# A two-layer encoder step on one core: loads and splits beside the attentions kept in program order, later marks, two more pairs of keys moved, a longer lead

## The chip, the core and the metric

The kernel runs on one core of a Trainium2 chip. The metric is device time in microseconds (us) from start to end of one launch, less being better. The core has a matrix engine (PE; its weight loads are listed as PEld), three elementwise engines (DVE, ACT, POOL), and SP, whose queue issues most DMA transfers. Every engine runs its own instruction stream in order, and semaphores tie the streams together. All engines share the on-chip memory SBUF; matmuls write to PSUM.

## What is computed

Two layers over 2048 prompt frames and 64 sample frames, width 1024, 16 heads of 64. Layer A attends over a band of chunks with softmax, layer B over all earlier frames with stick-breaking weights. Cut to the core of the reference:

```python
h = rms_norm(x, norm_a);  q, k, v, gate = split(h @ w_in_a, 4)
s = q @ k.T * SCALE + rel_bias;  p = softmax(where(mask, s, NEG_INF))   # band: own chunk + 8 before
x = x + ((p @ v) * silu(gate)) @ w_out_a
kb, vb = split(rms_norm(x, norm_kv) @ w_kv, 2)                          # shared by layer B
q, gate = split(rms_norm(x, norm_b) @ w_in_b, 2)
z = q @ kb.T * SCALE                                                    # strictly causal
log_fail = where(mask, log_sigmoid(-z), 0)
later = flip(cumsum(flip(log_fail))) - log_fail
w = where(mask, exp(log_sigmoid(z) + later), 0)
x = x + ((w @ vb) * silu(gate)) @ w_out_b
y = rms_norm(x, norm_f)
```

The sample frames also attend to cached keys and values, and the new keys and values are outputs too.

## The kernel before

**Precision.** All products are made from float32 values that are split in a high and a low part, each in the form that PE takes at full rate, and summed over three matmuls: high times high, high times low, low times high. So every operand costs a pass on ACT (the high part, a rounded copy) and one on DVE (the low part, the difference). These passes are the *splits* or *cuts*.

**Stages.** (1) Projection A makes k, q, v, gate of layer A: `ps_t` matmuls with the weights `wh`, `wl`, from 50 us to 750 us. (2) Attention A goes over eight head pairs in two halves of the frames, 763 to 1330 us; (3) the last output tiles of layer A (`ps_o`) run to 1455 us. (4) Projections for the shared keys and values and for layer B follow, to 2060 us. (5) Attention B (`z`, `f`, scans, `wt`, `acc`), 2070 to 3250 us. (6) The last output tiles of layer B.

**Attention.** Scores `z` are made by PE. In A, DVE adds the bias and takes the maximum, ACT makes the exponential `s`; in B, ACT makes `f`, POOL and DVE scan it to `s`. PE turns the weights over (`wt`), ACT and DVE split them (`ph`, `pl`), and PE multiplies them with the values (`acc`). One such round over a tile is a *beat* of the class `Beat`.

**Work beside the attention.** PE would wait for the elementwise engines in an attention, so `Beat` puts other matrix work between the beats, one *step* (six matmuls) at a time, `RATE` steps a beat: first *late jobs* (`late_job`), the projections of the second half of the frames for head pairs named in `DEFER` (tiles `lraw`, `lwh`, `lwl`, `ps_j`); then the splits of the output weights (`w_out_steps`: `woraw` to `big`); then the output tiles (`out_tile`: it loads the attention's output `og` and the residual `xr`, splits `og` in `oh` and `ol`, multiplies with the output weights in `ps_o`). Each has parts *ahead* (load and cuts), products, and parts *behind*. `Beat.lead(n)` runs n products before the first beat. An output tile may start when its frames' sums are written, which `when_summed` marks some beats later. A late job's load is traced with the first product of the job before it, and its cuts, each of `STEP` = 2 of eight blocks, with the products of that job's second half.

**What sets the order.** The program is traced once, and the tile framework then orders each engine's stream by itself, by its own estimate of when things are ready. A class `InOrder` can tie an instruction behind the one traced before it on the same engine (`keep_in_program_order`), but only while its flag `on` is set, and in this kernel it never is. The queue of SP holds the loads of q (L427), keys (L442), values (L448), the writes of the attention's output (L529), `lraw` (L641), `woraw` (L707), `og` (L736) and `xr` (L738).

**Between the layers.** `normed` loads a tile `xt`, squares it into a scrap tile `junk` on ACT, whose sum gives `rstd`; the scaled tile is transposed into `ps_tr` and split into `x_own`, which `ps_v` multiplies. `junk` takes its buffer from the pool tag of the residual `xr` (2 buffers).

Of the kernel before, what the change touches and what calls it, by code (L numbers as in the profile page):

```python
# [38 lines left out]

SAMPLE = {(1, 0): [4, 3], (3, 2): [2, 1, 0]}  # L40

DEFER = dict(a=[("k", 6), ("k", 7)], b=[(k, hp) for k in "gq" for hp in range(HP)])

RATE = dict(a=0.4, b=0.3)
LAG = dict(a=2, b=5)

LEAD = dict(a=8, b=8)
HOLD = dict(a=1, b=2)

STEP = 2  # L50
TOK = [(t * P, min(P, T - t * P)) for t in range((T + P - 1) // P)]

HALF = NP // 2
# [18 lines left out]
class InOrder:  # L72


    def __init__(self, tc):
        self.tc, self.on = tc, False

    def engine(self, engine):
        outer = self
# [17 lines left out]
def encoder_step(ctx: ExitStack, tc: tile.TileContext, a: dict, o: dict):  # L97
    nc = tc.nc
    order = InOrder(tc)
    dve, act, gps, pe = (order.engine(x) for x in (nc.vector, nc.scalar, nc.gpsimd, nc.tensor))  # L100
    mm = pe.matmul

    cpool = ctx.enter_context(tc.tile_pool(name="consts", bufs=1))
    dram = ctx.enter_context(tc.tile_pool(name="scratch", bufs=1, space=DRAM))
# [86 lines left out]
    def projections(L, x_of, begin, w_v, cv, gv, out_v, jobs, first, prompt, sample, stages):  # L191
        with (
# [1 line left out]
            tc.tile_pool(name=f"pp_{L}", bufs=1, space=PSUM) as psum,  # L194
        ):


            x_own = [xpool.tile([P, NK, HALF + m], F32R, name=f"x_own{i}") for i, m in enumerate((2 * NS, NS))]
            x_big = big_pair()
            xs = [x_own, x_big]  # L200
            with tc.tile_pool(name=f"v_{L}", bufs=2) as pool:

                def normed(t, scale=gps.tensor_scalar):
                    r0, n = TOK[t]
                    xt = pool.tile([P, D], F32, name="xt", tag="xt", bufs=3)
                    nc.sync.dma_start(xt[:n], x_of(t))
                    junk = opool.tile([P, D], mybir.dt.bfloat16, name="junk", tag="xr", bufs=2)
                    r = rstd_of(pool, xt, n, junk)
                    scale(xt[:n], xt[:n], r[:n], 1.0, ALU.mult, ALU.mult)
                    ps = psum.tile([P, NK, P], F32, name="ps_tr", tag="tr", bufs=1)  # L210
                    for k in range(NK):
                        flip(ps[:, k, :n], xt[:n, k * P : (k + 1) * P])
                    hf, c = spot(r0)
                    split(*(x[:, :, c : c + n] for x in xs[hf]), ps[:, :, :n])
                    if n == NS:
                        act.activation(x_own[0][:, :, NEW + NS :], f32(x_own[1][:, :, NEW:]), AF.Copy)

                seq = [t for gs_ in ORDER for g in gs_ for t in range(4 * g, 4 * g + 4)] + [len(TOK) - 1]
                if L == "a":
                    seq.sort()  # L220
                normed(seq[0], dve.tensor_scalar)
                begin()
                for half in range(2):
                    wh, wl = [], []
                    for k in range(NK):
                        raw = pool.tile([P, CH], F32, name="vraw", tag="vraw", bufs=2)
                        c = cv + half * CH
                        nc.sync.dma_start(raw, w_v[k * P : (k + 1) * P, c : c + CH])
                        h_ = pool.tile([P, CH], F32R, name="vwh", tag=f"vwh{k}", bufs=1)
                        l_ = pool.tile([P, CH], F32R, name="vwl", tag=f"vwl{k}", bufs=1)  # L230
                        act.activation(h_, raw, AF.Copy, scale=gv[:, k : k + 1])
                        dve.scalar_tensor_tensor(
                            l_, raw, gv[:, k : k + 1], f32(h_), ALU.mult, ALU.subtract
                        )
                        wh.append(h_)
                        wl.append(l_)
                    for i, t in enumerate(seq):
                        r0, n = TOK[t]
                        if half == 0 and i + 1 < len(TOK):
                            normed(seq[i + 1])  # L240
                        hf, c = spot(r0)
                        xh, xl = xs[hf]
                        ps = psum.tile([P, CH], F32, name="ps_v", tag="mm", bufs=5)
                        out = ps[:n]
                        if n == NS:
                            for k in range(NK):
                                both = x_own[0][:, k, NEW:]
                                mm(ps, both, wh[k], start=(k == 0), stop=False)
                                mm(ps, both, wl[k], start=False, stop=(k == NK - 1))
                            out = pool.tile([P, CH], F32, name="vn", tag="vn", bufs=2)[:n]  # L250
                            act.activation(out, ps[NS:], AF.Copy)
                            dve.tensor_tensor(out, ps[:n], out, ALU.add)
                        else:
                            mm3(
                                out,
                                lambda k: xh[:, k, c : c + n],
                                lambda k: xl[:, k, c : c + n],
                                lambda k: wh[k],
                                lambda k: wl[k],
                            )  # L260
                        if L == "a":
                            vs = pool.tile([P, 8, 2, DH], F32R, name="vs", tag="vs", bufs=2)
                            src = out.rearrange("p (h d) -> p h d", d=DH)
                            split(vs[:n, :, 0, :], vs[:n, :, 1, :], src)
                            nc.scalar.dma_start(
                                f32(lay[L]["v"][r0 : r0 + n, half * 8 : half * 8 + 8]),
                                f32(vs[:n]).rearrange("p h s d -> p h (s d)"),
                            )
                        dst = out_v(t)
                        if dst is not None:  # L270
                            vn = pool.tile([P, CH], F32, name="vn", tag="vn", bufs=2)
                            act.activation(vn[:n], out, AF.Copy)
                            cols = slice(half * CH, half * CH + CH)
                            nc.sync.dma_start(dst[:, cols], vn[:n])
                            if L == "b":
                                nc.scalar.dma_start(vraw[1 + r0 : 1 + r0 + n, cols], vn[:n])
# [358 lines left out]
    def late_job(L, kind, w, c0, g, hp, x2, psum, first, prompt):  # L635
        st = {}

        def load():
            st["raw"] = opool.tile([P, NK, P], F32, name="lraw", tag="og", bufs=1)
            c = c0 + hp * P  # L640
            nc.sync.dma_start(st["raw"], w[:, c : c + P].rearrange("(k p) c -> p k c", p=P))  # L641
            st["wh"] = opool.tile([P, NK, P], F32R, name="lwh", tag="oh", bufs=2)
            st["wl"] = opool.tile([P, NK, P], F32R, name="lwl", tag="ol", bufs=2)

# [49 lines left out]
            rows = kind == "k" and HALF + c >= first  # L694
            behind.append([partial(out, c)] + ([partial(add_back, c), (2, partial(token_rows, c))] if rows else []))
        products = [partial(some, c, k0) for c in chunks for k0 in range(0, NK, STEP)]
        return [load] + [partial(cut, k0) for k0 in range(0, NK, STEP)], products, behind

    def w_out_steps(src, w):

# [2 lines left out]
        def load(k):  # L703
            if k < NK:
                tag = ("oh", "ol")[k % 2]
                raws[k] = opool.tile([P, D], F32, name="woraw", tag=tag, bufs=2)
                nc.sync.dma_start(raws[k], src[k * P : (k + 1) * P])  # L707

        def cut(k):
            if k == 0:  # L710
# [4 lines left out]
            del raws[k]  # L715

        return [
            ([partial(load, i) for i in range(3)] if k == 0 else [], [None], [[partial(cut, k), partial(load, k + 3)]])
            for k in range(NK)
        ]  # L720

# [8 lines left out]
    def out_tile(L, g, t, c0, n, psum, w, residual, done):  # L730
        st = {}

        def load():
            st["og"] = opool.tile([P, NK, P], F32, name="og", tag="og", bufs=1)
            src = lay[L]["o"][g][:, :, c0 : c0 + n].rearrange("k p t -> p k t")
            nc.sync.dma_start(st["og"][:, :, :n], src)  # L736
            st["xr"] = opool.tile([P, D], F32, name="xr", tag="xr", bufs=2)
            nc.sync.dma_start(st["xr"][:n], residual(t))  # L738
            st["oh"] = opool.tile([P, NK, P], F32R, name="oh", tag="oh", bufs=2)
            st["ol"] = opool.tile([P, NK, P], F32R, name="ol", tag="ol", bufs=2)  # L740

# [34 lines left out]

        products = [partial(some, c, k0) for c in range(0, D, CH) for k0 in range(0, NK, STEP)]
        cuts = [partial(cut, k0) for k0 in range(0, NK, NK // 2)]
        return [load] + cuts, products, [[partial(out, 0)], [partial(out, CH), finish]]

    class Beat:

# [66 lines left out]
        def lead(self, n):  # L849
            while n > 0 and (self.now or self.beside):  # L850
                n -= 1
                self.ready = 0
                self.step()

        def products(self):
            while self.held and self.held[0][0] + self.hold <= self.clock:
# [46 lines left out]

        def when_summed(self, what):

            self.marks.append((self.blocks[-1][0] + 2 + self.hold, what))

        def end(self):
            while self.tiles or self.blocks or self.held or self.marks:
                self.beat()  # L910
            while self.now or self.beside:
                self.ready = 0
                self.step()
# [483 lines left out]
```

## Time and profile before

| | |
|---|---|
| median of 3 runs | 3362.42 us (3362.26 to 3369.03) |
| the profiled execution | 3363.2 us, of which its span is 3361.4 us (1.8 us lie around the span) |
| busy: PE, PEld | 3232.5 us (96%), 2801.8 us (83%) |
| busy: DVE, ACT, POOL | 1896.1 us (56%), 1723.1 us (51%), 1282.4 us (38%) |
| DMA | 643.30 MB, mean 191 GB/s |

The shares are means over stages with different limits. In the projections PE alone is busy, in the attentions all engines are. A matmul's busy time includes its pipeline, so that a PE that shows as busy without a break can still be short of its best rate; the spacing of the starts shows that rate. The granted clock (PEclk) is the share of full speed that PE was given in a stretch; its two levels are 2.4 and 1.2 GHz.

### The profile page before, as it was taken

To read this page: it belongs to the slowest core of one execution; us is meant where nothing else is said; L and a number is where in the kernel's file an instruction comes from. 1 tells how busy PE (TensorE), PEld (TensorE's weight loads), DVE (VectorE), ACT (ScalarE), POOL (GpSimd) and SP (SyncE) were. 2 spreads that over 40 slices of the span, in tenths; PEclk is the share of its full clock that TensorE was granted. 3 is DMA by queue.
4 is the path that set the end of the run, shared out by engine and by line. 5 is a ranking of instruction groups with operands and counts; after the bars stand their busy time and mean duration, and the time that the engine had idled before them with its cause. 6 is when DMAs were issued, how large, how long until landed. Compare 5 with 4: busy or idle time off the path is not lost.

```text
span 3361.4 us, 53483 instructions
## 1 busy us (share of the span) xinstructions
PE 3232.5 (96%) x17928; PEld 2801.8 (83%) x17928; DVE 1896.1 (56%) x3815; ACT 1723.1 (51%) x3716; POOL 1282.4 (38%) x1929
## 2 busy tenths in 40 slices
PE   8999999998999999999999999999999999999998
PEld 6889999986888888878889998778788787888777
DVE  3224431116886776322033333888888889888773
ACT  4323322226996776233144433666666676666661
POOL 2002210004774454021044200444476767777760
PEclk9999999998999999999999999999999999999999
DMA  5459984248998875544399857666735564445523
GB/s 188 140 176 362 338 318 155 95 146 258 253 241 221 240 215 151 188 138 137 106 338 352 294 184 226 178 186 189 192 103 140 155 181 127 129 128 152 139 89 110
DMA packets 454409, 643.30 MB, mean 191 GB/s; under 512 B 49733, under 2 KB 269925, under 8 KB 454134
## 3 DMA queue, kind: packets, MB, share of 16 engines
q1 hardware_dynamic: 394678, 588.75, 57.0%
q10 hardware_dynamic: 59456, 51.13, 4.7%
q8 instruction: 143, 2.34, 0.3%
q14 instruction: 132, 1.08, 0.1%
HBM read 388.85 MB, written 250.90 MB: 190 GB/s over the span
## 4 chain that ended last, share of the span: by engine, by line
PE 60%; DVE 7%; ACT 4%; DMA 3%; issue 3%; POOL 1%; SPq 0%; ACTq 0%; POOLq 0%; DVEq 0%
PE ps_o L86 10%; PE acc L86 10%; PE ps_t L86 10%; PE z L86 9%; PE wt L86 8%; PE ps_v L86 6%; PE ps_j L86 5%; DVE s L86 3%; DVE pl L86 2%; ACT ph L86 1%; ACT s L86 1%; DMA o_a<-ot 1%; ACT f L86 0%; DVE ol L86 0%; PE ps_tr L86 0%
## 5 line engine op out<-in xcount | busy, mean ns | idle before, releaser
L86 DVE TENSOR_TENSOR pl<-wt,ph 128x512 fp32r<-128x512 f32 (+1 forms) x864 | 551.8, 654 | 135.8 <-ACT ph L86 132.3
L86 ACT ACTIVATE ph<-wt 128x512 fp32r<-128x512 f32 (+1 forms) x864 | 483.7, 577 | 200.3 <-PE wt L86 183.4
L86 PE MATMUL wt<-ident,s 128*128 128x128 f32 x3472 | 552.6, 276 | 21.0 <-DVE pl L86 11.7
L86 PE MATMUL ps_t<-x_own,wh 128*128 128x362 f32 (+1 forms) x2304 | 569.9, 328 | 0.0
L86 PEld LDWEIGHTS wt<-ident,s 128*128 128x128 f32 x3472 | 418.5, 141 | 94.0 <-DVE pl L86 14.4
L86 ACT ACTIVATE f<-z 128x512 f32<-128x512 f32 (+4 forms) x680 | 355.3, 535 | 223.4 <-PE z L86 132.7
L86 POOL TENSOR_TENSOR s<-f,s 128x256 f32<-128x256 f32 x416 | 363.4, 874 | 122.0 <-DVE s L86 108.7
L86 PEld LDWEIGHTS ps_t<-x_own,wh 128*128 128x128 f32 x2304 | 404.8, 188 | 1.9
L86 PE MATMUL acc<-ph,vt 128*128 128x512 f32 (+3 forms) x1088 | 376.8, 381 | 20.5 <-ACT ph L86 14.3
L86 PE MATMUL acc<-pl,vt 128*128 128x512 f32 (+3 forms) x1088 | 368.3, 372 | 27.2 <-DVE pl L86 25.4
L86 PE MATMUL z<-kt,q 128*128 128x512 f32 (+3 forms) x1280 | 376.2, 381 | 11.3 <-ACT f L86 10.1
L86 PE MATMUL ps_t<-x_own,wl 128*128 128x362 f32 (+1 forms) x1152 | 377.4, 328 | 0.0
L86 POOL TENSOR_SCALAR s<-s,rc 128x640 f32<-128x640 f32 (+5 forms) x264 | 195.5, 748 | 469.6 <-DVE rc L86 419.0
L86 PE MATMUL ps_o<-big,oh 128*128 128x512 f32 x1088 | 338.8, 394 | 0.3 <-DVE pl L86 0.3
L86 POOL TENSOR_TENSOR two<-f 128x256 f32<-128x256 f32 x416 | 265.7, 641 | 168.4 <-ACT f L86 158.2
L86 DVE TENSOR_TENSOR_SCAN s<-two,s,own 128x256 f32<-128x256 f32 x408 | 299.6, 738 | 47.6 <-POOL two L86 41.9
L86 PE MATMUL ps_t<-big,wh 128*128 128x512 f32 x960 | 298.3, 391 | 0.0
L86 PEld LDWEIGHTS z<-kt,q 128*128 128x128 f32 x1280 | 220.3, 191 | 47.0 <-ACT f L86 23.8
L86 PEld LDWEIGHTS acc<-pl,vt 128*128 128x128 f32 x1088 | 196.2, 191 | 69.3 <-DVE pl L86 53.7
L86 PEld LDWEIGHTS acc<-ph,vt 128*128 128x128 f32 x1088 | 200.1, 192 | 46.6 <-ACT ph L86 21.0
L86 PEld LDWEIGHTS ps_o<-big,oh 128*128 128x128 f32 x1088 | 203.3, 189 | 42.0 <-DVE pl L86 0.9
L86 PEld LDWEIGHTS ps_t<-x_own,wl 128*128 128x128 f32 x1152 | 216.3, 188 | 0.1
(142 smaller groups left out, 5487.1 us busy)
## 6 DMA issues: line engine op xcount, KB each, us to landing
vt<-v_b SPq DMA_DIRECT2D x80, 512.0 KB, 5.1
v_b<-vs SPq DMA_DIRECT2D x64, 512.0 KB, 5.5
q<-q_a SPq DMA_DIRECT2D x128, 256.0 KB, 6.2
q<-q_b SPq DMA_DIRECT2D x128, 256.0 KB, 4.2
vt<-v_a SPq DMA_DIRECT2D x48, 512.0 KB, 8.1
kt<-k_b SPq DMA_DIRECT2D x96, 256.0 KB, 5.7
keys<-k_a SPq DMA_DIRECT2D x80, 256.0 KB, 6.7
v_a<-vs ACTq DMA_DIRECT2D x32, 512.0 KB, 2.7
```

The lines of the kernel that those rows point to most:

```text
L86: ins = op(*args, **kwargs)
```

## The change

Five edits are made at once.

- The loads and cuts of the late jobs, of the output weights and of the output tiles are wrapped in `in_place`: while an attention runs behind its lead (`order.amid`), each such instruction is tied behind the one traced before it on its engine, SP's queue included. Instructions that are not wrapped may still be moved past it.
- `SETTLE` = 5: an output tile is released five beats later.
- `DEFER["a"]`: the keys of head pairs 4 to 7 (before 6 and 7) have their second half in late jobs beside attention A and not in projection A. The counts of PE's instructions show it: 96 `ps_t` matmuls of 512 columns less, 96 `ps_j` more, PE's total unchanged at 17,930.
- `LEAD["b"]` is 14 products (before 8).
- `junk` gets a buffer of its own. The two 64-frame rests that the sample tile's product takes are copied by POOL into a tile `x_new` (two copies) and no longer by ACT into a wider `x_own`.

```diff
-DEFER = dict(a=[("k", 6), ("k", 7)], b=[(k, hp) for k in "gq" for hp in range(HP)])
+DEFER = dict(a=[("k", hp) for hp in (4, 5, 6, 7)], b=[(k, hp) for k in "gq" for hp in range(HP)])
-LEAD = dict(a=8, b=8)
+LEAD = dict(a=8, b=14)
+SETTLE = 5
...
+    def in_place(what):
+        def pinned():
+            was, order.on = order.on, order.amid
+            what()
+            order.on = was
+        return pinned
+    sp = order.engine(nc.sync)
...
-                    junk = opool.tile([P, D], mybir.dt.bfloat16, name="junk", tag="xr", bufs=2)
+                    junk = pool.tile([P, D], mybir.dt.bfloat16, name="junk", tag="junk", bufs=1)
...
-                        act.activation(x_own[0][:, :, NEW + NS :], f32(x_own[1][:, :, NEW:]), AF.Copy)
+                        x_new.append(opool.tile([P, NK, P], F32R, name="x_new", tag="ol", bufs=2))
+                        for i in range(2):
+                            gps.tensor_copy(x_new[0][:, :, i * NS : i * NS + NS], f32(x_own[i][:, :, NEW:]))
...
-            nc.sync.dma_start(st["raw"], w[:, c : c + P].rearrange("(k p) c -> p k c", p=P))
+            sp.dma_start(st["raw"], w[:, c : c + P].rearrange("(k p) c -> p k c", p=P))
...
-        return [load] + [partial(cut, k0) for k0 in range(0, NK, STEP)], products, behind
+        return [in_place(x) for x in [load] + [partial(cut, k0) for k0 in range(0, NK, STEP)]], products, behind
...
-            ([partial(load, i) for i in range(3)] if k == 0 else [], [None], [[partial(cut, k), partial(load, k + 3)]])
+            (
+                [in_place(partial(load, i)) for i in range(3)] if k == 0 else [],
+                [None],
+                [[in_place(partial(cut, k)), in_place(partial(load, k + 3))]],
+            )
...
-        return [load] + cuts, products, [[partial(out, 0)], [partial(out, CH), finish]]
+        return [in_place(x) for x in [load] + cuts], products, [[partial(out, 0)], [partial(out, CH), finish]]
...
+            order.amid = True
...
-            self.marks.append((self.blocks[-1][0] + 2 + self.hold, what))
+            self.marks.append((self.blocks[-1][0] + 2 + self.hold + SETTLE, what))
...
+            order.amid = False
```

How this moves the instructions is seen in the streams. The first place is ACT's stream where attention A begins its second half, at the first output tile (`oh` is the high part that is cut from `og`). Before:

```order
L86 ACTIVATE ph_10012<-wt_10007 128x512
L86 ACTIVATE otmp_9979<-acc_9934 64x512
L86 ACTIVATE ot_9883<-acc_9934 64x512
L86 ACTIVATE ph_10034<-wt_10029 128x512
L86 ACTIVATE oh_9852<-og_9848 128x512 x2
L86 ACTIVATE ph_10061<-wt_10056 128x512
L86 ACTIVATE s_10131,sm_10166<-s_10131,mn_10136 128x640
```

Now, at the cut of the same tile:

```order
L89 ACTIVATE s_10367,sm_10387<-s_10367,mn_10372 128x640
L89 ACTIVATE ph_10288<-wt_10283 128x512
L89 ACTIVATE s_10414,sm_10452<-s_10414,mn_10417 128x576
L89 ACTIVATE ph_10304<-wt_10299 128x512
L89 ACTIVATE oh_10024<-og_10020 128x512 x2
L89 ACTIVATE otmp_10296<-acc_10210 64x512
L89 ACTIVATE ot_10174<-acc_10210 64x512
```

The last sum that the load reads leaves ACT as `ot_9683` before and as `ot_9727` now. It is the 722nd row of ACT's stream before and the 729th now, and the cut is the 741st before and the 768th now: 18 rows stood between them, and 38 do now. On SP's queue the write of that sum, two or three other loads and the load of `og` still follow each other (rows 479 to 482 before, 483 to 487 now).

The second place is ACT's stream in attention B where one late job ends and the cuts of the next (`lwh`, eight blocks) come. Before:

```order
L86 ACTIVATE ph_22271<-wt_22268 128x256
L86 ACTIVATE f_22278<-z_22275 128x128
L86 ACTIVATE lwh_22546<-lraw_22544,g_b_77 128x128 x4
L86 ACTIVATE sg_22483<-ps_j_22215 128x512
L86 ACTIVATE lwh_22546<-lraw_22544,g_b_77 128x128 x3
L86 ACTIVATE f_22289<-z_22286 128x256
L86 ACTIVATE lwh_22546<-lraw_22544,g_b_77 128x128
L86 ACTIVATE ph_22316<-wt_22311 128x512
```

Now, two of the four pieces of one job:

```order
L89 ACTIVATE f_22577<-z_22574 128x128
L89 ACTIVATE lwh_22188<-lraw_22186,g_b_77 128x128 x2
L89 ACTIVATE f_22605<-z_22602 128x256
L89 ACTIVATE sp_22715<-ps_j_22486 128x512
L89 ACTIVATE total1_21085<-acc_22529 128x128
L89 ACTIVATE ph_22598<-wt_22593 128x512
L89 ACTIVATE f_22621<-z_22618 128x384
L89 ACTIVATE ph_22614<-wt_22611 128x256
L89 ACTIVATE f_22631<-z_22628 128x512
L89 ACTIVATE lwh_22188<-lraw_22186,g_b_77 128x128 x2
```

The eight cuts stood within ten rows and now stand in four pairs, seven to nine rows apart; on DVE the low parts `lwl` follow the same pattern.

The third place is ACT's stream between the layers, where the last output tiles of A end and `normed` begins. Before:

```order
L86 ACTIVATE oh_15508<-og_15504 128x4x64 x2
L288 DMA wraw_17086<-in_w_kv 128x8x128
L86 ACTIVATE wh_17088<-wraw_17086,g_kv_76 128x128 x8
L86 ACTIVATE junk_15620,ss_15621<-xt_15618 128x1024
L86 ACTIVATE ol_15509<-ps_o_15560 64x512
L86 ACTIVATE junk_15689,ss_15690<-xt_15687 128x1024
```

Now:

```order
L89 ACTIVATE oh_14728<-og_14724 128x512 x2
L89 ACTIVATE oh_15048<-og_15044 128x512 x2
L89 ACTIVATE junk_15664,ss_15665<-xt_15662 128x1024
L89 ACTIVATE vwh_15685<-vraw_15683,g_kv_76 128x512
L89 ACTIVATE vwh_15691<-vraw_15689,g_kv_76 128x512
L89 ACTIVATE junk_15733,ss_15734<-xt_15731 128x1024
```

The first `junk` stood behind the cuts of the very last output tile (`oh_15508`, the sample's); it now stands behind those of the second of the tiles that are cut after the attention, with eight tiles' cuts still to come.

## Rows read from the trace of the kernel before

**Rows 1.** Busy time by stretch: length, then PE, PEld, DVE, ACT, POOL, granted clock.

```profile
200.00:740.00 540.00, 539.87 (x2905) 494.94 (x2904) 163.61 (x402) 157.83 (x393) 54.37 (x49) 1.00 0.66 235
...
800.00:840.00 40.00, 31.39 (x167) 26.15 (x167) 29.48 (x73) 30.75 (x69) 20.89 (x21) 0.87 0.79 245
840.00:1000.00 160.00, 148.75 (x1014) 134.32 (x1013) 134.82 (x416) 151.73 (x362) 117.05 (x142) 0.99 0.92 247
...
2127.00:2423.00 296.00, 279.78 (x1648) 236.11 (x1647) 256.31 (x454) 196.08 (x448) 131.77 (x224) 0.99 0.70 190
...
3180.00:3240.00 60.00, 56.09 (x311) 42.70 (x310) 53.64 (x84) 42.07 (x84) 49.17 (x94) 1.00 0.29 84
```

**Rows 2.** What PE waited for over the span: total us, times, longest.

```profile
PE acc L86 <- DVE pl L86: 25.4, 48, 2.7
...
PE z L86 <- DMA q<-q_a: 5.5, 1, 5.5
```

**Rows 3.** Timeline of SP, ACT and PE at attention A's first output tile.

```profile
1008.10 0.37 SPq L736 DMA_DIRECT2D og<-o_a  x1
...
1012.22 1.15 ACT L86 ACTIVATE oh<-og 128x512 fp32r<-128x512 f32 x2 [6.24 <-DMA og<-o_a]
...
1013.91 0.80 PE L86 MATMUL acc<-ph,vt 128*128 128x256 f32 x2 [5.54 <-ACT ph L86]
1014.50 1.05 PE L86 MATMUL ps_o<-big,oh 128*128 128x512 f32 x2
...
1015.78 1.05 PE L86 MATMUL ps_o<-big,oh 128*128 128x512 f32 x2
...
1019.56 0.63 PE L86 MATMUL ps_o<-big,oh 128*128 128x512 f32 x2
...
1020.25 0.63 PE L86 MATMUL ps_o<-big,oh 128*128 128x512 f32 x2
```

**Rows 4.** Groups of ACT and of DVE from 800 to 840 us: the output weights' splits.

```profile
L86 ACT ACTIVATE big<-woraw 128x512 fp32r<-128x512 f32 x16 | 9.1, 623 | 3.0 <-DMA woraw<-in_w_out_a 3.0
...
L86 DVE TENSOR_TENSOR big<-woraw,big 128x512 fp32r<-128x512 f32 x16 | 12.2, 800 | 1.1 <-ACT big L86 1.1
```

**Rows 5.** Tile `lwh` from 2060 us: duration in ns (min/median/max), first and last start.

```profile
L86 ACT ACTIVATE lwh<-lraw,g_b x120: 383/389/405, 2065.8 to 2670.5; 128x128 fp32r<-128x128 f32 x120
L86 DVE SCALAR_TENSOR_TENSOR lwl<-lraw,g_b,lwh x120: 321/344/1369, 2066.2 to 2672.1; 128x128 fp32r<-128x128 f32 x120
```

**Rows 6.** Stretches of low granted clock, columns as in rows 1.

```profile
787.00:794.00 7.00, 3.66 (x17) 3.69 (x18) 2.68 (x8) 3.84 (x10) 1.28 (x2) 0.53 1.08 286
...
1459.00:1466.00 7.00, 5.71 (x23) 4.36 (x23) 1.56 (x3) 3.09 (x4) 1.29 (x3) 0.56 0.47 128
2088.00:2095.00 7.00, 5.39 (x14) 4.20 (x15) 5.21 (x12) 4.32 (x11) 4.52 (x10) 0.52 1.09 312
```

**Rows 7.** Timeline of ACT and of PE between the layers.

```profile
1452.07 1.06 ACT L86 ACTIVATE junk<-xt 128x1024 bf16<-128x1024 f32 x1 [1.56 <-DVE wl L86]
...
1458.89 1.10 PE L86 MATMUL ps_tr<-ident,xt 128*128 128x128 f32 x8 [3.38 <-POOL rstd L86]
```

**Rows 8.** Timeline of ACT and of PE at the start of attention B.

```profile
2086.63 2.44 ACT L86 ACTIVATE lwh<-lraw,g_b 128x128 fp32r<-128x128 f32 x8 [4.51 <-DMA lraw<-in_w_in_b]
...
2089.61 1.65 PE L86 MATMUL z<-kt,q 128*128 128x512 f32 x3 [5.25 <-ACT f L86]
```

**Rows 9.** Ten us before and after each of 13 bursts of cuts, columns as in rows 1.

```profile
2161.30:2171.30 10.00, 10.00 (x53) 8.39 (x52) 7.08 (x12) 4.36 (x9) 2.12 (x4) 1.00 0.79 206
...
sum 130.00, PE 129.93 PEld 109.45 DVE 93.45 ACT 60.29 POOL 61.10; mean PE 9.99 PEld 8.42 DVE 7.19 ACT 4.64 POOL 4.70
...
2171.30:2181.30 10.00, 7.75 (x49) 6.17 (x49) 9.71 (x21) 8.68 (x23) 3.56 (x7) 1.00 0.43 134
...
sum 130.00, PE 114.78 PEld 91.98 DVE 123.77 ACT 113.84 POOL 69.07; mean PE 8.83 PEld 7.08 DVE 9.52 ACT 8.76 POOL 5.31
```

**Rows 10.** Timeline of ACT at one of these bursts.

```profile
2171.31 1.28 ACT L86 ACTIVATE lwh<-lraw,g_b 128x128 fp32r<-128x128 f32 x4 [1.60 <-PE ps_j L86]
```

More of the change, by code (lines that the diff above doesn't have):

```diff
@@ L75, in __init__ @@
     def __init__(self, tc):
-        self.tc, self.on = tc, False
+        self.tc, self.on, self.amid = tc, False, False
     def engine(self, engine):
@@ L195, in projections @@
         ):
-            x_own = [xpool.tile([P, NK, HALF + m], F32R, name=f"x_own{i}") for i, m in enumerate((2 * NS, NS))]
+            x_own = [xpool.tile([P, NK, HALF + NS], F32R, name=f"x_own{i}") for i in range(2)]
             x_big = big_pair()
@@ L201, in projections @@
             with tc.tile_pool(name=f"v_{L}", bufs=2) as pool:
+                x_new = []
                 def normed(t, scale=gps.tensor_scalar):
@@ L246, in projections @@
                             for k in range(NK):
-                                both = x_own[0][:, k, NEW:]
+                                both = x_new[0][:, k]
                                 mm(ps, both, wh[k], start=(k == 0), stop=False)
@@ L706, in load @@
                 raws[k] = opool.tile([P, D], F32, name="woraw", tag=tag, bufs=2)
-                nc.sync.dma_start(raws[k], src[k * P : (k + 1) * P])
+                sp.dma_start(raws[k], src[k * P : (k + 1) * P])
         def cut(k):
@@ L735, in load @@
             src = lay[L]["o"][g][:, :, c0 : c0 + n].rearrange("k p t -> p k t")
-            nc.sync.dma_start(st["og"][:, :, :n], src)
+            sp.dma_start(st["og"][:, :, :n], src)
             st["xr"] = opool.tile([P, D], F32, name="xr", tag="xr", bufs=2)
-            nc.sync.dma_start(st["xr"][:n], residual(t))
+            sp.dma_start(st["xr"][:n], residual(t))
             st["oh"] = opool.tile([P, NK, P], F32R, name="oh", tag="oh", bufs=2)
```

## The prediction

> **What bounds the kernel now.** I read the busy time by stretch first [rows 1]. In a projection PE is busy 539.87 of 540 us: there every matmul that is moved away gives its full time. In attention A beside which no matrix work is left to run (840 to 1000 us), ACT is busy 151.73 of 160 us and PE 148.75: ACT binds, PE is a little behind. In the first half of attention B (2127 to 2423 us) DVE has 256.31 of 296 us and PE 279.78. So each stage has another limit, and what an edit is worth is read in its own stage.
>
> The second view is the list of PE's waits [rows 2]. It is short: 25.4 us for DVE's `pl` in 48 pieces, and single long ones such as 5.5 us for a load of q. A PE that works 96% of the span can lose in two more ways that the list does not show: a low granted clock behind each long wait, and matmuls that start further apart than they could.
>
> The third view prices both, the timeline at the first output tile of A [rows 3]. From 1019.56 to 1020.25 three matmuls of 512 columns start: 0.23 us each at full clock. From 1014.50 to 1015.78 it is also three: 0.43 us each. That stretch is the one behind a wait of 5.54 us; the granted clock is 0.53, 0.56 and 0.52 of full in the three like it that I need (the lower level, 1.2 GHz, for most of 7 us) [rows 6].
>
> **The change part by part.** Negative numbers are time saved; in brackets are the bounds.
>
> *Keys of two more pairs.* Projection A loses 96 matmuls of 512 columns: 96 x 0.23 = 22.1 us, and nothing else runs in their place there. Attention A gets them back, with their splits. Two jobs bring ACT 16 pieces of `lwh`, at 0.32 us each when back to back (1.28 for four) [rows 10], and eight operations of 512 columns (the split and the copy back) at about 0.6 us as `big` has it [rows 4]: 10 us. In a stretch that ACT bounds, attention A grows by these 10 us; if PE bounds, by 22. ACT has 95% and PE 93% in the stretch [rows 1], so I take 14, nearer to ACT's: 14 - 22 = **-8** (-12 to 0).
>
> *Splits of A's output weights.* They now come in one lump: from 800 to 840 us ACT spends 9.1 us on 16 of them, with a wait of 3.0 us for their load, and DVE 12.2 us [rows 4]; PE stands still 8.6 of these 40 us at a clock of 0.87 [rows 1], which costs some 4 us more. In program order they stand one by one over later pairs, where the lump's 12.6 us go. But ACT, which has 5% free there, has to take their 9.1 us all the same: 9 - 12.6 = **-4** (-8 to 0).
>
> *First output tile of A.* On SP's queue the load of `og` stands until the last sum is written and goes out at 1008.10. ACT's cut `oh` waits for it 6.24 us in front of the `ph` that PE needs, PE stands 5.54 us and then makes its next matmuls at 0.43 us: twelve from 1014.50 to 1019.56, 5.06 us where 12 x 0.23 = 2.8 would do [rows 3]. Together 5.5 + 2.3 = 7.8 us. Now 38 rows of ACT stand between the last sum and the cut, 18 before. One of the extra 20 takes 0.6 us or more, so that 12 us pass, twice the wait. The load itself may still stand at the head of SP's queue, but it holds back only loads for later rounds. **-7** (-8 to 0).
>
> *Between the layers.* `junk` starts at 1452.07, just ahead of the last matmuls of A, since its buffer is that of the residual; PE waits 3.38 us at 1458.89 for the chain behind it [rows 7] and gets 0.56 of the clock over the next 7 us, 0.44 x 7 x 5.71/7 = 2.5 us [rows 6]. With a buffer of its own, and eight tiles' cuts behind it in ACT's stream, this is over long before: **-6** (-6 to 0). The two copies on POOL have that whole projection to hide in; without this cover they cost under 2 us.
>
> *Start of B.* ACT cuts the third job's eight blocks at 2086.63, after 4.51 us of waiting for their load, while `f` stands behind; PE waits 5.25 us [rows 8] and then has 0.52 of the clock for 7 us [rows 6], 0.48 x 5.39 = 2.6 us. The load is now ahead of most loads that stood before it, and the cut comes in pairs behind several `f`. Against it, six more products stand in front: 36 x 0.23 = 8.3 us, which later stretches save; where PE is not the bound they save less, at worst nothing. 7.8 saved, about half of it spent: **-4** (-8 to 0).
>
> *Cuts in attention B.* This is the largest term. Thirteen times (the first at 2126.9, the last at 2667.9 us) eight `lwh` and eight `lwl` come together when the last product of the job before is done; ACT waits for that product [rows 10]. In the 10 us ahead of them PE is busy 129.93 of 130 us, in the 10 us behind 114.78, while DVE climbs to 123.77 [rows 9]: PE has neither the beside work (not cut yet) nor the attention's (DVE and ACT are cutting). That is 15.2 us. Now a job is cut in four pairs during the second half of the job before, when PE has its matmuls. By weight loads instead of matmuls the loss is (109.45 - 91.98) / 109.45 x 130 = 20.7 us. I take **-15** (-21 to 0, the latter being a rival below). The Trainium skill (Perfetto Trace Analysis, Identifying the Most-Contended Engine) calls the matmul's busy share a poor measure and goes by weight loads; by its rule this term would be -20.7 and the whole 3314. No more than the row is used here, since the mix of matmuls differs before and behind.
>
> *Later marks.* Five beats later, an output tile is missing a while as filler, at the end above all: from 3180 to 3240 us, where nothing stands beside the attention, PE is busy 56.09 of 60 us [rows 1]. A third of such a stretch more is **+1.5** (0 to +4).
>
> Sum: -8 - 4 - 7 - 6 - 4 - 15 + 1.5 = -42.5 us. The profiled execution took 3363.2 us, 0.8 more than the median; 3362.4 - 42.5 is **3320 us**.
>
> **The rivals.**
>
> *DVE keeps the bound in B, ACT in A.* The bursts' loss is then only spread. DVE is at 86.6% in the first half of B [rows 1], and its work does not become less. A piece of `lwl` takes 321 ns at least and 1369 at most [rows 5]; if pieces that stand alone among POOL's work meet the long form more often, each time costs 1.05 us, and fifteen times over 104 pieces eat the term. The new keys in A would likewise cost what they save. Without these two (15 and 8 us): 3363.2 - 19.5 - 0.8 = 3343 us. For it speaks that DVE, ACT and PE are all within 15% of each other; against, that PE is full ahead of each burst and DVE at 93.45 of 130 there [rows 9], so that there is room in time. The Trainium skill (SBUF, Who interferes with whom) says that a DVE operation with two inputs in SBUF blocks against a POOL operation that reads SBUF, which fits the spread of `lwl` and speaks for this rival; how often they meet after the change no row shows.
>
> *The other side: pinned loads block SP's queue.* A pinned load may not be passed over by the loads traced ahead of it, so a load of `og`, `lraw` or `woraw` whose buffer or data is late stands at the head, and loads of q, keys and values behind it come late. The price is the one in the trace: PE waits 5.5 us for q [rows 2], in a stretch of which the clock is 0.53 [rows 6], 3.66 x 0.47 = 1.7 us more, so 7 us each. Six such stalls use up the gain, seven and more make it slower; with one at every second of the 20 late jobs it is 10 x 7 - 42.5 = +27, 3390 us. For it: the queue already stood before `og` until 1008.10. Against: that stand itself cost ACT's cut, not a load behind it, and PE waits for DMA hardly at all [rows 2].
>
> *Nothing but the moves.* The framework's order had found most of these places a use, and what is gained at one stall is lost at the next (the chain of waits closes up): 3360 us. Against it speaks that the stalls at 1013, 1459 and 2089 us end on single named releasers.
>
> *More.* All terms at their far bound: -12 - 8 - 8 - 6 - 8 - 21 = -63, 3299 us.
>
> **How the numbers follow.** Forecast (3308 to 3334) 0.55; DVE and ACT bound (to 3353) 0.22; more 0.08; nothing 0.07; blocked queue 0.08. The range from 3299 to 3353 leaves out the last two cases in full and little of the others. A change under 0.2% (6.7 us) can't be told from none in this kernel: faster 0.55 + 0.22 + 0.08 = 0.85, same 0.07, slower 0.08.
>
> **What would show it.** Projection A ends 22 us earlier. From 800 to 840 us PE stands less than 4 us, and the lump is not found again at a later place. No wait over 3 us stands at the first `ps_o` of A, at the first `ps_tr` between the layers, or at the third job of B. The pieces of `lwl` stand apart, and PE's busy share has no dip to 0.8 every 44 us from 2127 to 2680. The forecast is wrong if PE's waits for DVE's `pl` grow in B instead of shrinking, if attention A grows by over 20 us, or if waits for DMA appear among PE's.

## The result and the profile after

The changed kernel takes 3322.76 us (median of four runs, 3318.66 to 3326.92) against 3363.78 us for the kernel before on the same chip (the three runs above and a fourth): ratio 0.9875, interval 0.9858 to 0.9892. The profiled execution, the fastest of the four, spans 3316.9 us, 44.5 less than the one of before; by the medians the gain is 41 us. The forecast was 3320 us. The total agrees; the terms under it agree less, and most of what follows is on that.

Stage lengths in us from the two timelines. A stage begins with PE's first instruction of it, and an attention ends with PE's last scores `z` of the prompt frames, so that its last weights and sums count with the output tiles:

| stage | before | after | change |
|---|---|---|---|
| up to the first `ps_j` (projection A) | 753.3 | 729.1 | -24.2 |
| attention A | 575.1 | 569.5 | -5.6 |
| its last output tiles, with the gap behind them | 130.5 | 135.4 | +4.9 |
| projections for B | 609.2 | 608.3 | -0.9 |
| lead of attention B | 9.6 | 17.3 | +7.7 |
| first half of attention B (eight head pairs) | 345.1 | 327.5 | -17.6 |
| second half of attention B | 822.2 | 809.6 | -12.6 |
| last output tiles, end | 116.4 | 120.2 | +3.8 |

The busy time by stretch of the kernel after (columns as in rows 1): a head pair of attention A, then the first of B's first half, and the other seven together.

```profile
867.40:904.50 37.10, 29.39 (x164) 25.58 (x163) 29.59 (x78) 30.23 (x69) 19.75 (x23) 0.82 0.80 229
...
2059.60:2100.60 41.00, 36.91 (x196) 30.79 (x195) 31.68 (x52) 23.16 (x53) 13.00 (x25) 0.92 0.76 217
2100.60:2387.10 286.50, 280.22 (x1664) 238.57 (x1663) 262.23 (x455) 197.46 (x448) 133.87 (x225) 1.00 0.72 198
```

And of the kernel before, the same two parts of attention B:

```profile
2077.70:2127.10 49.40, 42.19 (x211) 33.63 (x210) 32.45 (x55) 24.54 (x56) 14.25 (x28) 0.90 0.82 225
2127.10:2422.80 295.70, 279.48 (x1646) 235.83 (x1644) 256.04 (x453) 195.82 (x447) 131.47 (x223) 0.99 0.70 190
```

The seven pairs are 9.2 us shorter with more matmuls in them, and DVE now works 262.23 of 286.50 us there, 92%. The row of attention A shows that the lump of the output weights' splits, which stood at 800 to 840 us [rows 1], is still a lump: it has moved to 867 to 905 us, PE stands 7.7 us of 37.1, and the clock is 0.82 (0.87 at 800 to 840 us before).

The list of PE's waits after (compare rows 2):

```profile
PE acc L89 <- DVE pl L89: 16.6, 45, 1.3
...
PE acc L89 <- DMA vt<-v_b: 4.7, 1, 4.7
```

The waits for `pl` fell from 25.4 to 16.6 us, and the wait for q is gone. A new one for values (`vt`) stands once, a sign that the prediction had named against itself. It may be the blocked queue of the second rival, but no row shows a tied load in front of it, and run 10 below, with the same ties, waits 0.2 us for `vt`.

The timeline at the first output tile of A (compare rows 3) and, between the layers, the three rows that answer to rows 7:

```profile
1010.92 0.72 PE L89 MATMUL ps_o<-big,oh 128*128 128x512 f32 x2 [0.52 <-ACT oh L89]
...
1433.07 0.68 DVE L89 TENSOR_TENSOR xr<-ps_o,ol 64x512 f32<-64x512 f32 x1
...
1433.96 1.83 PE L89 MATMUL ps_tr<-ident,xt 128*128 128x128 f32 x8 [2.34 <-issue]
```

PE's wait at the output tile is 0.52 us, where it was 5.54. Between the layers PE still waits 2.34 us (3.38 before), although `junk` now runs long before: its first three start between 1333.6 and 1340 us. The row of DVE shows who comes last: its read of the last `ps_o` ends at 1433.75 us, and `ps_tr` starts 0.2 us later. The same row of the kernel before, behind the row of POOL that the profile names there as the releaser:

```profile
1457.33 0.98 POOL L86 TENSOR_TENSOR rstd<-ms,nhalf 128x1 f32<-128x1 f32 x1
1458.00 0.68 DVE L86 TENSOR_TENSOR xr<-ps_o,ol 64x512 f32<-64x512 f32 x1
```

DVE's read ends at 1458.68, and `ps_tr` started at 1458.89 [rows 7]. POOL's `rstd` had ended 0.4 us before that read, at 1458.31. The stream's order shows the first `ps_tr` waiting for DVE, ACT, POOL and several DMA queues at once, so the last of these decides, and in both kernels the last that these rows show is DVE. That it is the last of all is read from the times and was not tried by a run.

At the start of B (compare rows 8) PE still waits 3.44 us, where it was 5.25:

```profile
2073.35 0.60 ACT L89 ACTIVATE sp<-ps_j 128x512 fp32r<-128x512 f32 x1 [3.86 <-DMA gate_b<-sg]
...
2074.49 0.69 PE L89 MATMUL z<-kt,q 128*128 128x128 f32 x2 [3.44 <-ACT f L89]
```

The third job's cuts are no longer in front of `f`; another row of ACT is, the split of a late job's result (`sp`), and that one waits for a write of `gate_b` to land. The clock over the 7 us from 2074 us is 0.63 (0.52 before).

### The profile page after: what moved, and what is told of

It reads as the page before. It is cut to its first block, busy times and chain, and to the rows that moved or that the text cites. A ratio compares the mean times of both kernels' runs of the same rounds, so it can differ in the third digit from the quotient of the medians.

```text
span 3316.9 us, 53520 instructions
## 1 busy us (share of the span) xinstructions
PE 3214.8 (97%) x17928; PEld 2795.3 (84%) x17928; DVE 1916.7 (58%) x3831; ACT 1723.0 (52%) x3730; POOL 1282.8 (39%) x1933
## 3 DMA queue, kind: packets, MB, share of 16 engines
q8 instruction: 143, 2.34, 0.3%
## 4 chain that ended last, share of the span: by engine, by line
PE 81%; DVE 8%; ACT 4%; DMA 4%; issue 2%; POOL 1%; SPq 0%; POOLq 0%; ACTq 0%; DVEq 0%
PE ps_t L89 25%; PE ps_v L89 11%; PE ps_o L89 11%; PE acc L89 10%; PE z L89 8%; PE wt L89 8%; PE ps_j L89 6%; DVE s L89 3%; DVE pl L89 3%; PE ps_tr L89 1%; ACT ph L89 1%; ACT s L89 1%; DVE lwl L89 1%; DMA q<-q_a 1%; PE ps_n L89 0%
## 5 line engine op out<-in xcount | busy, mean ns | idle before, releaser
L89 PE MATMUL ps_t<-x_own,wh 128*128 128x362 f32 (+1 forms) x2304 | 570.2, 328 | 0.0
L89 PE MATMUL acc<-pl,vt 128*128 128x512 f32 (+3 forms) x1088 | 364.1, 368 | 17.4 <-DVE pl L89 16.6
L89 PE MATMUL ps_t<-big,wh 128*128 128x512 f32 x896 | 278.5, 391 | 0.0
```

Source lines behind the costliest of these rows:

```text
L89: ins = op(*args, **kwargs)
```

## The experiments

Two theories went into the first four. P: the ties to program order carry the gain, as the prediction's sum has it. K: the keys and the longer lead carry it, the ties only rearrange. Ratios are to the kernel before on the same chip.

**1. Without the ties.** `in_place` returns its argument unchanged.

```diff
-        return [in_place(x) for x in [load] + cuts], products, ...
+        return [load] + cuts, products, ...
```

(and the same at the late jobs and the output weights). 

> The changed kernel without the ties to program order; the keys of four pairs, the longer lead, the later marks and the own buffer of junk stay. Theory P (the ties carry most of it): attention B's first half loses its 9 to 17 us again, with bursts of eight cuts in a row and PE's busy share near 0.8 behind each, and a wait of 5 us stands again at the first output tile of A; about 3350 us. Theory K (keys and lead carry it, the ties only rearrange): about 3325 us, with the first half of B as short as in the changed kernel.

Measured: 3342.41 us, 0.9935 (0.9921 to 0.9950): 20 us slower than the changed kernel, between the two theories, so the ties are worth about half of the gain, with the other edits there. Attention A is 11 us longer, and the wait at its first output tile is back, as P had it:

```profile
1004.34 1.15 ACT L89 ACTIVATE oh<-og 128x512 fp32r<-128x512 f32 x2 [5.94 <-DMA og<-o_a]
...
1006.03 0.80 PE L89 MATMUL acc<-ph,vt 128*128 128x256 f32 x2 [5.24 <-ACT ph L89]
```

The delay of five beats is still in this run. Without the ties it moves nothing here: 18 rows of ACT stand between the last sum and the cut, as before. The first half of B, in the same two parts as above:

```profile
2071.00:2118.80 47.80, 38.47 (x206) 31.41 (x206) 32.90 (x54) 25.55 (x56) 12.98 (x26) 0.93 0.68 196
2118.80:2410.10 291.30, 283.14 (x1658) 236.64 (x1657) 253.91 (x454) 195.72 (x445) 131.66 (x225) 1.00 0.70 195
```

The start costs 6.8 us more than with the ties. The seven pairs, with their cuts in bursts of eight again, take 291.3 us and not 286.5: the bursts are worth 4.8 us here, not 15. A part of what the ties save goes back: the same 64 pieces of `lwl` take DVE 31.5 us in the first half with the ties and 21.1 us without. This is the spread of `lwl` that the first rival had spoken of.

**2 to 4. The ties alone, in the kernel before:** all of them; on the late jobs only; on the output tiles only.

```diff
-DEFER = dict(a=[("k", hp) for hp in (4, 5, 6, 7)], ...
-LEAD = dict(a=8, b=14)
-SETTLE = 5
+DEFER = dict(a=[("k", 6), ("k", 7)], ...
+LEAD = dict(a=8, b=8)
+SETTLE = 0
```

(with the old `junk` and `x_own`, and for 3 and 4 the ties taken off the other groups). 

> The kernel before with the ties alone. Theory P: 3330 to 3338 us, PE's wait at the first output tile of A gone (6 to 8 us), eight pairs of the first half of B together 12 to 20 us shorter than before. Theory K: 3355 to 3363 us. The blocked queue of the prediction's rivals would show as waits of PE for q or keys of 5 us and more: over 3363 us.

 

> The kernel before with the ties on the late jobs' loads and cuts alone. Theory P: attention B's first half is 12 to 20 us shorter, attention A as before: 3343 to 3350 us. Theory K: within 3 us of before, the bursts' loss only spread out.

 

> The kernel before with the ties on the output tiles' loads and cuts alone. Theory P: the second half of attention A gains the stall of 7 to 8 us, up to 15 if the later tiles gain too, and B nothing: 3348 to 3356 us. Theory K: the load of og at the head of SP's queue holds up what is behind it, 3363 us or more.

Measured: 3351.28 us, 0.9961 (0.9946 to 0.9975); 3355.16 us, 0.9981 (0.9969 to 0.9994); 3352.40 us, 0.9971 (0.9960 to 0.9982). All are faster than before, by 13, 6 and 10 us; the first two gain far less than P asked. The third lies in P's range, but not by P's way: in its profiled execution (3361.24 us, the slowest of its ten) attention A is as long as before, 575.1 us, and PE waits 4.49 us for `oh`. With the ties alone, 22 rows of ACT stand between the last sum and the cut. The first half of B shows what the late jobs' ties do: 345.2 and 344.8 us with the late jobs tied, 345.1 before. The cuts stood in pairs, and nothing was gained. PE also had a new wait, here in the run with the late jobs alone tied:

```profile
PE ps_j L89 <- ACT lwh L89: 6.1, 1, 6.1
```

So P fell for attention B: spreading the cuts alone pays nothing, and spreading them with a lead of 14 pays the 4.8 us of run 1.

**5 to 7. One edit taken back at a time.** `DEFER["a"]` = pairs 6 and 7; `SETTLE` = 0; `LEAD["b"]` = 8.

```diff
-DEFER = dict(a=[("k", hp) for hp in (4, 5, 6, 7)], ...   # run 5
-SETTLE = 5                                               # run 6
-LEAD = dict(a=8, b=14)                                   # run 7
+DEFER = dict(a=[("k", 6), ("k", 7)], ...
+SETTLE = 0
+LEAD = dict(a=8, b=8)
```

> The changed kernel with the keys of head pairs 4 and 5 back in projection A (two late jobs there as before). The prediction's term: projection A 22 us longer, attention A 14 us shorter, 3331 us in all. If attention A took them free of charge: 3345 us. If ACT and PE there charge their full price: 3323 us.

 

> The changed kernel with the output tiles released at the beats of before. Theory E (the delay costs at the ends): the last output tiles of A and of B each 3 to 6 us shorter, no wait over 3 us comes back at the first tile since the ties alone keep the cut away from its load; 3313 to 3318 us. Theory W (the delay is what removes the waits): PE waits 5 us again at the first tile of A, and the gain at the ends is lost: 3323 us or more.

 

> The changed kernel with 8 products ahead of attention B. Two runs with the ties and this lead had PE wait 6 to 7 us for the third job's cuts. Theory T (ties and lead need each other): this wait is back and the first half of B is 6 to 10 us slower than its fill explains: 3329 to 3335 us. Theory L (a longer lead only moves products to the front): within 3 us of the changed kernel.

Measured: 3332.78 us, 0.9913 (0.9899 to 0.9928); 3334.05 us, 0.9917 (0.9903 to 0.9932); 3341.06 us, 0.9937 (0.9922 to 0.9952). By the ratios the edits are worth 13, 14 and 21 us, each with an uncertainty of several us. The keys: the first `ps_j` starts at 751.6 us and not at 729.1, 22.5 us, and attention A is 13.8 us shorter, nearly the prediction's 22 and 14 (attention A alone varies by up to 6 us, see the last section).

The marks: theory E fell, W holds in part. With `SETTLE` = 0 and the ties, ACT's cut waits for its load again, and PE for the cut:

```profile
1005.00 1.15 ACT L89 ACTIVATE oh<-og 128x512 fp32r<-128x512 f32 x2 [3.85 <-DMA og<-o_a]
...
1005.69 0.77 PE L89 MATMUL ps_o<-big,oh 128*128 128x512 f32 x2 [3.55 <-ACT oh L89]
```

Neither edit alone keeps cut and load apart. With the ties alone 22 rows of ACT stand between the last sum and the cut, with the delay alone (run 1) 18, with both 38. Attention A is 17 us longer than in the changed kernel and its last tiles 6.5 shorter, since half a tile's products (24 matmuls) went into the attention instead: 11 us net. The 3.55 us are a part of them; where the rest comes from was not tried.

The lead: 21 us are more than either theory had, and far more than the 7.0 us that PE waits for `lwh` at the start, a wait that theory T had right. Head pairs 5 to 8 take 42 to 45 us, with the same number of products beside them (48 matmuls each) as those of 40 to 43 us in the changed kernel.

**8. The low parts on POOL.**

```diff
-            scaled_split(st["wh"][:, ks], st["wl"][:, ks], st["raw"][:, ks], g[:, ks])
+            raw, wh, wl = st["raw"], st["wh"], st["wl"]
+            for k in range(k0, k0 + STEP):
+                gps.tensor_scalar(raw[:, k], raw[:, k], g[:, k : k + 1], 1.0, ALU.mult, ALU.mult)
+            act.activation(wh[:, ks], raw[:, ks], AF.Copy)
+            gps.tensor_tensor(wl[:, ks], raw[:, ks], f32(wh[:, ks]), ALU.subtract)
```

> The changed kernel with the low parts of the late jobs' weights made by POOL (it scales the raw block in place, ACT copies it, POOL subtracts) and not by DVE. If DVE binds the first half of attention B, its 2.4 us and more for each job come off the path there: eight pairs 8 to 20 us shorter, 3303 to 3315 us. If PE's own pace binds, within 3 us of the changed kernel; if POOL's longer operations come late, slower, with PE waiting for wl.

Measured: 3315.40 us (3314.97 to 3317.15), 0.9861 (0.9844 to 0.9877): the fastest median of all. But the kernel before is 2.9 us faster in this comparison too, and the intervals of the two ratios overlap, so that the gain of 5 us over the changed kernel that the ratios give is not shown. Pairs 2 to 8 of the first half:

```profile
2108.70:2390.10 281.40, 277.74 (x1662) 237.40 (x1661) 239.07 (x398) 190.37 (x420) 170.47 (x308) 1.00 0.74 201
```

DVE has 23 us less to do than in the changed kernel (239.07 for 262.23), and the seven pairs are 5.1 us shorter; the first pair is 3.0 us longer, so that all eight gain 2.2 us and not the 8 to 20 expected. DVE binds a part of that time; PE, busy 277.74 of 281.40, stands close behind.

**9 and 10. Other leads.** `LEAD["b"]` = 16 and 11, all else as in the changed kernel. Theory C: the lead is cover for the third job. Theory F: it sets where in a head pair the steps and cuts of all later jobs fall. A late job has eight products, and each of the later head pairs of the first half takes in eight, so this place stays the same from pair to pair, and 16 gives that of 8.

```diff
-LEAD = dict(a=8, b=14)
+LEAD = dict(a=8, b=16)   # run 9; 11 in run 10
```

> The changed kernel with 16 products ahead of attention B, two whole late jobs, so that a job begins at the same place of a head pair as with 8 but with twice the time for the third job's load. Theory C (the lead is cover for the third job's load and cuts): as good as 14, 3319 to 3326 us. Theory F (14 sets where in a head pair the steps and cuts fall): head pairs 5 to 8 of the first half take 43 to 45 us as with a lead of 8 and not 40 to 41: 3330 to 3338 us.

 

> The changed kernel with 11 products ahead of attention B: the third job's load and cuts have less cover than with 14 and more than with 8, and a job's first products fall elsewhere in a head pair than with either. Theory C: PE waits for lwh or f by 2 to 5 us at the start and the later pairs take 40 to 41 us: 3324 to 3329 us. Theory F: the later pairs differ from both.

Measured: 3349.95 us, 0.9965 (0.9951 to 0.9978), and 3318.16 us, 0.9871 (0.9849 to 0.9893). Two more products in the lead cost 27 us (30 by the ratios), three fewer cost nothing. C fell: with 16 the time was not that of 14, and with 11 PE has no wait for `lwh` or `f` over 1.1 us at the start. F holds for the later pairs. The rows of pairs 6 to 8 with a lead of 16 and, in the second fence, of 8 are nearly the same rows:

```profile
2279.70:2322.80 43.10, 41.24 (x246) 35.20 (x245) 38.60 (x69) 28.45 (x65) 18.96 (x32) 1.00 0.70 196
2322.80:2367.40 44.60, 41.23 (x239) 34.36 (x238) 39.88 (x67) 27.96 (x65) 19.30 (x32) 1.00 0.67 186
2367.40:2412.20 44.80, 41.27 (x244) 34.80 (x242) 38.84 (x67) 28.68 (x65) 19.32 (x33) 1.00 0.68 183
```

```profile
2271.40:2314.40 43.00, 41.13 (x245) 35.15 (x244) 38.49 (x68) 28.39 (x65) 18.96 (x32) 1.00 0.69 196
2314.40:2359.10 44.70, 41.31 (x240) 34.39 (x240) 39.96 (x67) 28.01 (x65) 19.32 (x33) 1.00 0.67 186
2359.10:2403.80 44.70, 41.16 (x244) 34.73 (x242) 38.80 (x67) 28.63 (x65) 19.27 (x33) 1.00 0.67 183
```

Head pairs 5 to 8 have 48 matmuls of late jobs each in every run, so that their time can be compared across runs. First without the ties, lead 8 (the kernel before) and lead 14 (run 1); then with them, lead 8 (run 7) and lead 14 (the changed kernel):

```profile
2249.60:2422.80 173.20, 165.83 (x970) 140.23 (x968) 149.40 (x266) 114.13 (x259) 76.16 (x129) 0.99 0.71 192
2244.20:2410.10 165.90, 162.55 (x953) 135.76 (x952) 145.80 (x261) 112.41 (x256) 75.39 (x129) 1.00 0.71 196
2229.20:2403.80 174.60, 164.12 (x958) 137.72 (x956) 155.71 (x264) 112.69 (x257) 76.58 (x129) 1.00 0.68 187
2223.80:2387.10 163.30, 159.67 (x950) 136.40 (x949) 149.48 (x260) 112.74 (x256) 76.53 (x129) 1.00 0.71 197
```

The lead is worth 7 us without the ties and 11 with them; the ties are worth 3 us at lead 14 and cost 1 at lead 8. Leads of 16 and 11 give 174.4 and 166.6 us with the ties. PE's waits for `pl` over the whole span follow the lead as well: 22 to 32 us in the six kernels with 8 or 16, the one of before among them, and 16.6 to 18.6 in the four with 14 in which DVE makes the low parts (16.7 without the ties).

This does not make all of the 27 us the lead's. Between the profiled executions with 14 and 16 lie 31 us: 11 in head pairs 5 to 8, 4 in the first four, 6 in the second half of B, 2 in the lead itself, and 9 in attention A and its last tiles, whose order is the same in both.

What the place does is seen inside a pair. Five-us stretches of the second of these, lead 8 (columns as in rows 1):

```profile
2324.40:2329.40 5.00, 5.00 (x39) 4.57 (x38) 5.00 (x10) 4.39 (x12) 2.89 (x6) 1.00 0.30 94
2329.40:2334.40 5.00, 4.31 (x26) 3.15 (x25) 4.94 (x9) 2.74 (x9) 4.53 (x7) 1.00 1.02 273
2334.40:2339.40 5.00, 3.68 (x18) 2.55 (x18) 5.00 (x10) 3.87 (x9) 2.68 (x6) 1.00 0.85 237
2339.40:2344.40 5.00, 3.98 (x17) 3.04 (x18) 3.13 (x6) 1.41 (x4) 3.79 (x6) 1.00 0.81 215
```

and the same stretches for the tile `ps_j` alone (PE only: busy, clock, DMA):

```profile
2324.40:2329.40 5.00, 0.00 (x0) 1.00 0.30 94
2329.40:2334.40 5.00, 0.00 (x0) 1.00 1.02 273
2334.40:2339.40 5.00, 0.00 (x0) 1.00 0.85 237
2339.40:2344.40 5.00, 3.26 (x14) 1.00 0.81 215
```

For 15 us no product of a late job stands beside the attention, DVE is full (14.94 us), three of the job's four pairs of cuts fall into just this time (`lwl` in pairs from 2327.5, 2332.7 and 2337.9 us), and PE falls to 3.68 of 5. Of the changed kernel's pair of 40.3 us, the weakest five us:

```profile
2283.90:2288.90 5.00, 4.46 (x29) 3.73 (x27) 5.00 (x8) 4.79 (x11) 3.32 (x7) 1.00 0.67 206
```

**11 and 12. Towards a better version.** Run 11 adds POOL's low parts (only while an attention runs), POOL's copies for A's output weights, and a slower rate for the splits of the output weights; run 12 is POOL's low parts, again only while an attention runs, with a lead of 11.

```diff
+                if L == "a":                                  # run 11
+                    gps.tensor_copy(hi, raw)
+                    dve.tensor_tensor(lo, raw, f32(hi), ALU.subtract)
...
-            return 1.0 if product else 0.5
+            return 1.0 if product else self.pause             # 2.0 in A, 1.0 in B
...
-LEAD = dict(a=8, b=14)                                        # run 12
+LEAD = dict(a=8, b=11)
```

> The changed kernel with three moves: POOL makes the low parts of the late jobs' weights while an attention runs; in layer A POOL and not ACT makes the high part of the output weights; and the eight pieces of the output weights are let in at a slower rate (a piece counts as two products in A, one in B; before half of one). If ACT binds head pairs 4 to 7 of A, these four lose the lump of 10 to 13 us; with the 7 us of the POOL run before: 3303 to 3311 us. If the slower rate only delays the output tiles, the last tiles of A and B grow by as much: 3314 to 3320 us.

 

> The changed kernel with POOL making the low parts of the late jobs' weights while an attention runs (layer A's first job and B's first two, cut before, stay with DVE) and with 11 products ahead of attention B. If the two gains of 7 and 5 us add up: 3309 to 3314 us. If both live from the same slack of DVE in the first half of B, no more than the better one: 3315 to 3318 us. If the other place of the cuts spoils what POOL takes over: over 3320 us.

Measured: 3322.25 us, 0.9885 (0.9862 to 0.9908), and 3318.98 us, 0.9868 (0.9852 to 0.9885). Neither is shown to beat run 8; run 11 is above both of its ranges. In run 11 head pairs 5 to 8 of A take 117.5 us in sum (28.9, 31.3, 31.5, 25.8) where the changed kernel takes 112.4 (37.1, 26.7, 24.5, 24.1): the lump is gone, and nothing is gained. Whether the spreading or POOL's copies eat it was not tried apart, and 5 us are within what attention A varies by. In run 12 the two gains do not add up.

## Why the prediction was right, and where its steps were not

The time was met because errors of both signs cancelled; that the total agrees within 3 us is luck.

*Right.* The keys: 22 saved and 14 spent, measured 22.5 and 13.8. The stall at the first output tile: 5.54 us down to 0.52, by ties and delay together.

*Size wrong: "Cuts in attention B", -15.* I took the whole idle time behind the 13 bursts for their price. Run 1 has the bursts with the lead of 14, and its seven pairs lose 4.8 us by them; runs 2 and 3 spread the cuts at the old lead and gain nothing. The seven pairs did become 9.2 us shorter, but 4.4 of that stand in run 1 too, without the ties. The row that I read (PE 114.78 of 130 us behind the bursts, rows 9) showed two things at one place: the cuts, and that no product stands beside the attention there (`ps_j` runs 2.2 us of these 130, and 77.8 of the 130 ahead). The second is not cured by moving the cuts, and the rival "DVE keeps the bound" had a part right: DVE is at 92% now, and pieces of `lwl` that stand apart take it longer (31.5 us in the first half against 21.1 in run 1).

*Step failed: "Start of B", where the longer lead cost 4 us and hid a load.* The load is hidden, but PE still waits 3.44 us there, now behind `sp`, and the lead and the first head pair together take 58.3 us where they took 59.0, with 24 more matmuls of late jobs in them. What the longer lead did bring is elsewhere: against 8 it is worth 21 us (run 7), 11 of them in head pairs 5 to 8 through the place that it gives to every later job. I had counted the products that the lead moves and not where the rest then fall.

*Step failed: "Later marks", +1.5.* The ends did grow (5.9 and 3.9 us at the last `ps_o`), but run 6 shows 14 us gained: without the delay the cut waits for `og` again. I had put down only what the delay costs. The 38 rows of ACT that the term "First output tile of A" counts on need the delay and the ties; either alone leaves 18 or 22 and the wait. Where the rest of the 14 us comes from stays open.

*Step failed: "Splits of A's output weights", -4.* The lump moved on by three head pairs, behind the two added jobs, and nothing was saved. Its 16 copies on ACT now stand over 37 us (870.8 to 907.8) where they stood over 20, and PE stands 7.7 us in that head pair as it stood 8.6 before: further apart was not cheaper.

*Step failed: "Between the layers", -6.* The wait went from 3.38 to 2.34 us. Two releasers came within 0.4 us of each other, the later one being DVE's read of the last `ps_o` (by the rows; no run removed it), and only the named one was removed.

The second half of B is 12.6 us shorter, which no step foresaw, but it holds 696 matmuls of the beside work where it held 759: 63 x 0.23 = 14.5 us at the spacing of rows 3. So no gain is shown there; the products lie in the lead, in the first half and at the end.

The edits are not additive: taken back one at a time, ties, keys, marks and lead are worth 20, 13, 14 and 21 us, 68 in all, of a gain of 42 by the ratio.

## What to carry to other kernels

When work is fed in beside a loop at a fixed rate, look where in the loop's period it falls before counting how much of it there is: a stretch in which the elementwise engine is full and no matrix work stands beside it sets the price, and one number at the start shifts all later steps. Before taking a wait's time as a gain, look for a second releaser that ended close to the named one. And a stretch that is slow behind an event shows everything that happens there: run the event alone at another place before giving it the whole loss. And an edit that costs on its own can be what another needs: here a later release moved the cut only with the ties, and the ties alone hardly moved it.

## What was not expected of the hardware

Attention A of the changed kernel has the same order in runs 7, 9 and 10, and still took 570.2, 575.3 and 572.7 us (569.5 in the changed kernel itself): up to 6 us between profiled executions whose streams agree there. The first half of B, whose order is the same in the changed kernel and in run 5, agreed within 1 us (327.5 and 328.2).

POOL's copy of 128 x 512 into the form that PE takes at full rate had a mean of 668 ns in run 11, against 623 for ACT's `big` in rows 4; its difference of two 128 x 256 blocks had a median of 738 ns in run 8, and two of DVE's scaled differences (128 x 128) take 688 [rows 5].
